# Two attention query jobs made a pair of block sums in a hybrid decoder step

## The chip, the cores and the metric

The kernel runs on one core of one Trainium2 chip. A core has a matrix engine (TensorE, PE in the profile), a vector engine (VectorE, DVE), a scalar engine (ScalarE, ACT), a general engine (GpSimd, POOL) and a sync engine (SP) that issues most transfers. The metric is the device time of one execution in microseconds. Of the kernel before, three runs took 834.29, 834.73 and 835.82 us; the median is 834.73.

## The reference

One layer of a decoder with two branches is computed for a prompt of 1024 positions and for 8 samples of 4 positions each (32 sample positions). The width is 1024.

```python
h, gate = adaln_in(x, c, w_ada, b_ada, g_norm)          # normalised, conditioned rows
(mq, mk, mv, mi, mf, mo, mz, aq, ak, av, az, gm, ga) = split_in(h @ w_in)
y_m, C, n, m = mlstm_branch(mq, mk, mv, mi, mf, mo, mz, C0, n0, m0, b_i, b_f, g_mn)
q = partial_rope(aq.reshape(B, T, A_HEADS, A_HEAD_DIM), pos)
...
o = attn_prompt(q, k, v, sinks)     # window of 128, 8 query heads on 2 key heads of 64
y_a = o.astype(x.dtype) * jax.nn.silu(az)
u = jax.nn.sigmoid(gm) * (y_m @ w_mo) + jax.nn.sigmoid(ga) * (y_a @ w_ao)
x = x + gate * (u @ w_o)
```

The first branch has four heads of 128 with a matrix memory that is carried over chunks of 128 positions. The second is attention over a sliding window. Samples attend to a cache and have memories of their own. All data is float32, and the outputs are the rows, the states and the kept keys and values.

## The kernel before, in words

**Products in three parts.** Every large product of float32 is made from a high and a low part of both operands, in the form float32r: high by high, high by low, low by high. Weights are split into `wh` and `wl` when they have been loaded: ACT copies the high part and DVE subtracts.

**Plain jobs.** A plain job (`job`, with `job_part` and `piece`) makes 128 columns of `h @ w_in` for all 1056 positions. It takes the positions in pieces of 384, 384 and 288 and, for each, eight blocks of the inner dimension, three matmuls for each block. The list `order` says which jobs are plain: keys and values of attention (`ak`, `av`), its four query groups (`aq` 0 to 3), then the first head's `mq`, `mk`, `mv` and the second head's `mq`, and at the end of the kernel the products with `w_mo`. `queries(g)` is the plain job of a query group: its evacuation scales by 0.125, applies the rotation and stores the queries in DRAM (`qD`), and the last piece also fills the samples' queries in `qpad`.

**Pairs.** All other columns of `w_in` are made two jobs at a time (`Pair`, `block_products`). The two jobs' weights are four blocks and the prompt's rows are four blocks, and seven products of sums of such blocks replace eight. Each product is 4 blocks of the inner dimension x 3 matmuls of 512 columns. The sums of the rows' blocks (`t1` to `t4`) are formed once by the generator `sum_blocks`; the sums of weights' blocks are formed for each pair by DVE (`first_sums`, `split`). The products go in the order 1, 6, 2, 7, 5, 3, 4 in the first pair, and 5, 6, 2, 7, the next pair's 1, 3, 4 in the others. They accumulate in PSUM banks (`X`, `W`, `Y`, `Z`); product 6 goes on a bank `bw` that ACT has filled with a copy of the result of product 1, and products 7 and 4 on a bank `by`. Each finished quarter goes to `evac` of the pair's kind. The 32 samples are done apart: 16 small matmuls `smp` and one `smpo`. The kinds are `head_in` (4 pairs), `gate` (8), `query_gate` (2) and `head_gate` (4).

**Side work.** Between the matmuls of jobs and pairs, `side.tick()` lets in work of other kinds. Each kind is a generator that yields where it has to wait: the units of attention (`unit(g, b0)`, 16 of them, stream "a"; each has a visit of scores `sc`, one of transposes `pt` and one of outputs), the heads of the matrix memory (`head`, stream "m"), the samples' attention and heads (`sample_attention`, `sample_head`, stream "s"), the sums of blocks (stream "x"), and conditioning gates and output weights (`ada_gate`, `out_weights`, stream "g"). `Side` keeps a modelled time, and starts a step when its time has come and its class of PSUM banks has been free long enough. The banks are of four classes, g, a, b and o, two each; units take their scores' banks from a beside plain jobs and from o beside pairs.

**Order.** The order on TensorE is written out by hand: each matmul and transpose has a dependency on the one before (`mm` and `tr` call `in_order`). In the part of the program that matters here, DVE and ACT are placed by a scheduler, and then keep their queue's order. Transfers go out on SP's queue in the order of the program, stores some time after their data.

**Samples' heads.** After each second head, `sample_head` sums the partial results of two heads. It multiplies them with a constant (`C_S32`, 32 columns) into a bank `st`, copies the 32 rows, normalises, transposes each head into one half of a bank `sty`, and multiplies it into `gs`:

```python
for i, (g, _) in enumerate(tails):
    tr(ty[:, i], ns[:, i, 0:128], ident[:NS, :NS])
    V.tensor_scalar(gs[:, g], ty[:, i], gmn[:, g:g + 1], None, op0=ALU.mult)
```

**Output weights.** `out_weights` multiplies the rows of `w_out` with the gate and forms sums of blocks of them for the end of the kernel; it is started by `hook` at product 6 of the pair of number `OUT_WEIGHTS`, which is the second gate pair.

Of the kernel before, what the change touches and what calls it, by code (L numbers as in the profile page):

```python
# [14 lines left out]
AF = mybir.ActivationFunctionType  # L15
ALU = mybir.AluOpType
# [5 lines left out]
SEQ = 1024  # L22
NB = 8
NT = 4
NS = NB * NT
T = SEQ + NS
PITCH = 1088
NH = 4
# [4 lines left out]
KT = D // 128  # L33
# [4 lines left out]
C_END = 849  # L38
# [135 lines left out]
def body(tc, a):  # L174
    nc = tc.nc
    with ExitStack() as ctx:
# [11 lines left out]
        def pb(shape, name):  # L188
            return ps.tile(shape, F32, tag="b", bufs=2, name=name)

        def po(shape, name):
            return ps.tile(shape, F32, tag="o", bufs=2, name=name)

        def ht(shape, name, dt=F32):
            return sp.tile(shape, dt, tag="half", bufs=50, name=name)

        def sm(shape, name, bufs=3, dt=F32):
            return sp.tile(shape, dt, tag=name, bufs=bufs, name=name)
# [45 lines left out]
        def store(out, in_):  # L244
            due.append((side.now + 8.0, out, in_))
# [8 lines left out]
        def dma(out, in_, late=False):  # L254
            stores(in_.tensor)
            issue(out, in_, late)
# [10 lines left out]
        def mm(out, lhsT, rhs, start, stop, share=1, more=False):  # L267
            n = int(np.prod(rhs.shape[1:]))
            side.now += max(n, 250) / 2400 if rhs.dtype == F32R else max(n * 4 // share, 128) / 2400
            side.products += 1  # L270
            in_order(nc.tensor.matmul(out, lhsT, rhs, start=start, stop=stop, skip_group_check=more))  # L271

        def tr(out, in_, idn):
            side.now += 0.11
            side.products += 1
            in_order(nc.tensor.transpose(out, in_, idn))  # L276
# [43 lines left out]
        cst = cp.tile([128, C_END], F32, name="cst")  # L320
# [243 lines left out]
        order = []  # L564
# [345 lines left out]

        def sample_attention():
            qpad, vns, kTs = at["qpad"], at["vns"], at["kTs"]
            kc, vc = ([ht([128, 4, 128], f"{n}{u}") for u in range(2)] for n in ("kc", "vc"))
            smask = ht([128, 2, WIN + NS], "smask")
            sinkr = cp.tile([128, 1], F32, name="sinkr")
            for u in range(2):
                dma(kc[u], a["cache_k"][:, 4 * u:4 * u + 4])
                dma(vc[u], a["cache_v"][:, 4 * u:4 * u + 4])
            dma(smask, a["smask"])
            dma(sinkr, a["sink_rows"])  # L920
            yield 12.0, "b"
            for u in range(2):
                tq = pb([128, 4, 128], f"kctp{u}")
                for j in range(4):
                    tr(tq[:, j], kc[u][:, j], ident)
                S.copy(kc[u], tq)
                yield 3.0, "b" if u == 0 else "o"
            sc = po([128, 2, WIN + NS], "scs")
            for u in range(2):
                for w in range(4):  # L930
                    b = u * 4 + w
                    qb = qpad[:, b].rearrange("p k g t -> p (k g t)")
                    r = slice(32 * w, 32 * w + 32)
                    mm(sc[r, u, 0:WIN], qb, kc[u][:, w], start=True, stop=True)
                    mm(sc[r, u, WIN:], qb, kTs, start=True, stop=True)
            p = ht([128, 2, WIN + NS], "ps")
            mx = cp.tile([128, 2], F32, name="mxs")
            for u in range(2):
                V.tensor_tensor_reduce(p[:, u], sc[:, u], smask[:, u], 1.0, sinkr, ALU.add, ALU.max,
                                       accum_out=mx[:, u:u + 1])  # L940
            nmx = cp.tile([128, 4], F32, name="nmxs")
            V.tensor_scalar(nmx[:, 0:2], mx, -1.0, None, op0=ALU.mult)
            V.tensor_scalar(nmx[:, 2:4], nmx[:, 0:2], sinkr, None, op0=ALU.add)
            den = cp.tile([128, 2], F32, name="dens")
            for u in range(2):
                S.activation(p[:, u], p[:, u], AF.Exp, bias=nmx[:, u:u + 1], accum_out=den[:, u:u + 1])
            S.activation(nmx[:, 2:4], nmx[:, 2:4], AF.Exp)
            V.tensor_tensor(den, den, nmx[:, 2:4], op=ALU.add)
            V.reciprocal(den, den)
            for u in range(2):  # L950
                V.tensor_scalar(p[:, u], p[:, u], den[:, u:u + 1], None, op0=ALU.mult)
            yield 10.0, "b"
            pt = pb([128, 4, 128], "pts")
            for u in range(2):
                tr(pt[:, u], p[:, u, 0:WIN], ident)
                tr(pt[:NS, 2 + u], p[:, u, WIN:], ident)
            pT = kc[0]
            S.copy(pT[:, 0:2], pt[:, 0:2])
            V.tensor_copy(pT[:NS, 2:4], pt[:NS, 2:4])
            yield 7.0, "o"  # L960
            o = po([128, 2, 128], "os")
            for u in range(2):
                for w in range(4):
                    r = slice(32 * w, 32 * w + 32)
                    mm(o[r, u], pT[:, u, r], vc[u][:, w], start=True, stop=False, share=4)
                for w in range(4):
                    r = slice(32 * w, 32 * w + 32)
                    mm(o[r, u], pT[:NS, 2 + u, r], vns, start=False, stop=True, share=4)
            S.copy(p[:, :, 0:128], o)
            yield 4.0, "b"  # L970
            ot = pb([128, 2, 128], "ost")
            for u in range(2):
                tr(ot[:, u], p[:, u, 0:128], ident)
            for u in range(2):
                v4 = lambda t: t.rearrange("p (w k g t) -> p w k g t", k=2, g=4, t=NT)
                for kv, r in enumerate(half_rows):
                    V.tensor_copy(osm[r, :, 16 * u:16 * u + 16].rearrange("p g (w t) -> p w g t", t=NT), v4(ot[r, u])[:, :, kv])
            samples_done.append("a")


        yhD = [dp.tile([128, SEQ], F32, name=f"yhD{h}") for h in range(NH)]
# [54 lines left out]
        mD = [[dp.tile([128, SEQ], F32, name=f"{n}D{h}") for n in "qkv"] for h in range(NH)]  # L1036

        def head(h):
            an, wend, dec, fl = st["an"], st["wend"], st["dec"], st["fl"]
            C = [None]  # L1040
            w_ = {}
# [133 lines left out]
        def sample_head(h):  # L1175
# [64 lines left out]
                return  # L1240
            yield 3.0, "o"
            tot = po([128, 2, 129], f"st{h}")
            for i, (_, n4) in enumerate(tails):
                mm(tot[:NS, i], cst[:, C_S32:C_S32 + NS], n4, start=True, stop=True)
            ns = z[:NS, 0:258].rearrange("p (m e) -> p m e", e=129)
            S.copy(ns, tot[:NS])
            ssq = sm([NS, 2], "sssq", 2)
            for i in range(2):
                jk = sm([128, 128], "mjk", 2, BF16)
# [6 lines left out]
            for i in range(2):  # L1256
                V.tensor_scalar(ns[:, i, 0:128], ns[:, i, 0:128], d[:, i:i + 1], r[:, i:i + 1], op0=ALU.mult, op1=ALU.mult)
            yield 4.0, "b"
            ty = pb([128, 2, NS], f"sty{h}")
            for i, (g, _) in enumerate(tails):  # L1260
                tr(ty[:, i], ns[:, i, 0:128], ident[:NS, :NS])
                V.tensor_scalar(gs[:, g], ty[:, i], gmn[:, g:g + 1], None, op0=ALU.mult)
                samples_done.append(g)
            tails.clear()
            if h == NH - 1:
# [159 lines left out]
        def ahead(self, key, src, th):  # L1425
            self.held[key] = o = ht([128, 512], "ho")
            dma(o, src[:, HALF[th]])

        class head_in:
            names = lambda i: paired[i]  # L1430
            ahead = lambda self, i: None
# [155 lines left out]
                    W = filled(pg, "bw", X, j)  # L1587
                side.tick()

        order += [("ak", 0), ("av", 0)] + [("aq", g) for g in range(4)]  # L1590
        inner = [(n, h) for h in range(NH) for n in ("mq", "mk", "mv")]
        paired = list(zip(inner[4::2], inner[5::2]))
        order += inner[:4]
# [411 lines left out]
                    summed("t4", k, b21, t2, ALU.subtract)  # L2005
                    yield 2.4, ""

        pairs = [Pair(head_in, i) for i in range(len(paired))] + [Pair(gate, d) for d in range(KT)] + [Pair(query_gate, i) for i in range(2)] + [Pair(head_gate, h) for h in range(NH)]

        def hook(n, i):  # L2010
            if n == 0 and i in (6, 5):
                side.until(lambda: {6: "t2", 5: "t1"}[i] in formed)
            if i == 6:
                if pairs[n].kind is query_gate:
                    side.until(lambda: len(units_done) == 16)
                side.until(lambda: len(samples_done) >= {head_in: 0, gate: 0, query_gate: 1, head_gate: pairs[n].i + 2}[pairs[n].kind])
            if (n, i) == (OUT_WEIGHTS, 6):
                side.add("g", out_weights())
            if (n, i) in LOADS:
                side.add("x", att_sums(LOADS.index((n, i))))  # L2020
            if n == len(pairs) - 1:
                next(att, None)

        OUT_WEIGHTS = 5
        LOADS = [(len(pairs) - 2, 7), (len(pairs) - 1, 5)]
        work = block_products(pairs, hook)
        att = att_products()
        side.add("g", ada_gate())
        side.add("x", sum_blocks())
        blocks["t1"] = block(0, 1)  # L2030
        for g in range(4):
            queries(g)
        side.add("s", sample_attention(), "b")
        for h in range(NH):
            head_jobs(h)

# [337 lines left out]
```

## Time and profile before

| | |
|---|---|
| median of three runs | 834.73 us |
| the profiled execution | 832.12 us |
| its span, first to last instruction | 830.4 us |
| mean granted clock of TensorE | 0.997 |
| TensorE busy | 810.4 us |
| VectorE busy | 593.8 us |
| ScalarE busy | 420.5 us |
| share of the DMA engines' time, main queue | 54.1% |

Rows of the timeline have the start in microseconds, the duration, the engine and line, the operation with its tiles (out<-in) and, where the engine was idle before, for how long and what released it. Matmuls overlap: the distance of two starts is what one costs. Almost all matmuls stand on line 271 and all transposes on line 276, since helpers issue them; tiles tell them apart. A group's row has count, busy time, mean duration in ns and the idle time before it.

The main stages are: loading and normalising first, plain jobs up to about 209 us, the eighteen pairs up to about 640 us, then the output products of attention, the plain jobs with `w_mo` (690 to 735 us) and the final rows.

### The profile page before, as it was taken

The page shows a single profiled execution, that of the slowest core. Times are in us where ns is not written, and L with a number is a line of the kernel's source. Part 1 is how long each engine was busy: PE and PEld are TensorE (multiplying, and loading weights), DVE is VectorE, ACT ScalarE, POOL GpSimd, SP SyncE. Part 2 cuts the span into 40 slices and gives each one's busy share as a digit, 9 for nine tenths or more (in the row PEclk, how much of TensorE's full clock was granted, in tenths as well). Part 3 has the DMA queues.
Part 4 walks back from the last instruction along what each step waited for, and adds up shares of the span by engine and source line. Part 5 has one row for each costly group of instructions (what it writes and reads, how often), then busy time and mean ns, then how long its engine had stood idle before and what let it go on. Part 6 is the DMA issues. An engine that isn't in the chain of part 4 may idle for free. (4 is left out here: it accounts for less than half of the span.)

```text
span 830.4 us, 15038 instructions
## 1 busy us (share of the span) xinstructions
PE 810.4 (98%) x5129; PEld 669.3 (81%) x5129; DVE 593.8 (72%) x1479; ACT 420.5 (51%) x1030; POOL 67.2 (8%) x128
## 2 busy tenths in 40 slices
PE   6999999999999999999899999999999999999996
PEld 3779897888788788888788877887888789997775
DVE  4889886656656456475577785897569988974776
ACT  5664365555474564555455453544346654334343
POOL 0120000000000001000001000000002104250000
PEclk9999999999999999999999999999999999999998
DMA  9997766356436425479856345464336785643633
GB/s 334 378 357 238 184 201 213 118 150 217 143 111 189 114 85 150 140 240 286 268 188 205 120 141 155 143 203 142 103 117 196 230 288 172 212 146 122 202 109 108
DMA packets 106689, 153.96 MB, mean 185 GB/s; under 512 B 20448, under 2 KB 54368, under 8 KB 106580
## 3 DMA queue, kind: packets, MB, share of 16 engines
q1 hardware_dynamic: 100964, 142.25, 54.1%
q10 hardware_dynamic: 4176, 6.56, 2.2%
q0 software_dynamic: 1472, 4.20, 1.4%
q8 instruction: 40, 0.66, 0.3%
q14 instruction: 37, 0.30, 0.1%
HBM read 109.22 MB, written 44.75 MB: 185 GB/s over the span
## 5 line engine op out<-in xcount | busy, mean ns | idle before, releaser
L220 ACT ACTIVATE p<-p,nmx 128x256 f32<-128x256 f32 (+1 forms) x64 | 31.0, 486 | 12.4 <-DVE nmx L220 12.1
L271 PE MATMUL g_aq<-h_h,wh_aq 128*128 128x384 f32 (+1 forms) x96 | 32.2, 336 | 0.0
L271 PE MATMUL g_aq<-h_h,wl_aq 128*128 128x384 f32 (+1 forms) x96 | 30.9, 322 | 0.0
L271 PE MATMUL g_aq<-h_l,wh_aq 128*128 128x384 f32 (+1 forms) x96 | 30.8, 321 | 0.0
L271 PE MATMUL g_w_mo<-ym_l,wh_w_mo 128*128 128x384 f32 (+1 forms) x96 | 30.8, 321 | 0.0
L271 PE MATMUL g_w_mo<-ym_h,wh_w_mo 128*128 128x384 f32 (+1 forms) x96 | 30.8, 321 | 0.0
L271 PE MATMUL g_w_mo<-ym_l,wl_w_mo 128*128 128x384 f32 (+1 forms) x96 | 30.8, 321 | 0.0
L220 DVE CUSTOM_DVE_ANT_0 p<-sc,cst,sink 128x256 f32<-128x256 f32 (+1 forms) x64 | 26.2, 464 | 5.3 <-PE sc L271 5.2
L259 POOL DMA_DIRECT2D oD<-uqv x16 | 8.9, 554 | 183.2 <-ACT uqv L220 161.0
L220 DVE COPY p<-pt 128x512 f32<-128x512 f32 (+1 forms) x16 | 10.5, 657 | 13.6 <-PE pt L276 13.6
L271 PEld LDWEIGHTS g_aq<-h_h,wh_aq 128*128 128x128 f32 x96 | 18.0, 188 | 2.5 <-issue 1.5
L271 PEld LDWEIGHTS g_w_mo<-ym_l,wh_w_mo 128*128 128x128 f32 x96 | 18.0, 188 | 0.0
L271 PEld LDWEIGHTS g_aq<-h_l,wh_aq 128*128 128x128 f32 x96 | 18.1, 188 | 0.0
L271 PEld LDWEIGHTS g_w_mo<-ym_h,wh_w_mo 128*128 128x128 f32 x96 | 18.0, 188 | 0.0
L271 PE MATMUL sc<-ukv,uqv 64*128 64x256 f32 (+1 forms) x128 | 18.0, 390 | 0.0
L271 PEld LDWEIGHTS g_aq<-h_h,wl_aq 128*128 128x128 f32 x96 | 18.0, 188 | 0.0
L271 PEld LDWEIGHTS g_w_mo<-ym_l,wl_w_mo 128*128 128x128 f32 x96 | 18.0, 188 | 0.0
L220 ACT ACTIVATE p<-p,den 128x256 f32<-128x256 f32 (+1 forms) x32 | 14.5, 491 | 5.7 <-DVE den L220 5.6
L220 ACT ACTIVATE sq<-rows_h 128x512 f32<-128x512 f32 (+2 forms) x14 | 8.2, 582 | 17.8 <-issue 12.0
L220 DVE TENSOR_TENSOR et<-et,S 128x384 f32<-128x384 f32 (+1 forms) x12 | 6.1, 510 | 15.4 <-PE S L271 12.7
L271 PE MATMUL g_mq<-h_h,wh_mq 128*128 128x384 f32 (+1 forms) x48 | 16.8, 349 | 0.3 <-ACT mk L220 0.3
L276 PE MATMUL pt<-cst,p 128*128 128x128 f32 x120 | 16.4, 277 | 0.5 <-DVE mx L220 0.5
(2073 smaller groups left out, 2841.4 us busy)
## 6 DMA issues: line engine op xcount, KB each, us to landing
x<-xT SPq DMA_DIRECT2D x16, 256.0 KB, 5.6
early_h<-w_ada SPq DMA_DIRECT2D x8, 512.0 KB, 9.0
adar_ga<-w_ada SPq DMA_DIRECT2D x16, 256.0 KB, 4.0
wr_ga<-w SPq DMA_DIRECT2D x16, 256.0 KB, 2.9
wr_gm<-w SPq DMA_DIRECT2D x16, 256.0 KB, 3.6
taD<-gt SPq DMA_DIRECT2D x16, 256.0 KB, 2.2
tmD<-gt SPq DMA_DIRECT2D x16, 256.0 KB, 5.3
wor<-w_out SPq DMA_DIRECT2D x16, 256.0 KB, 5.1
```

Source lines behind the costliest of these rows:

```text
L220: ins = f(*args, **kw)
L259: ins = (eng or nc.sync).dma_start(out, in_)
L271: in_order(nc.tensor.matmul(out, lhsT, rhs, start=start, stop=stop, skip_group_check=more))
L276: in_order(nc.tensor.transpose(out, in_, idn))
```

## The change

Query groups 2 and 3 are no longer plain jobs. They are the first pair of a new kind, `att_in`, whose evacuation adds, shuffles, multiplies with 0.125 and the rotation's tables and stores the queries; it loads four tables of 128 x 512 for that. When both halves of a group are stored, its four units are added to the stream, so they come beside pairs. The samples' attention is started from this pair, waits until four units are done, loads the cached values later, and limits how many units run at a time to two while it runs and to three after it. A `head` waits until its gates' values exist and `t1` has been formed. In `sample_head` the state sums take 104 columns of the constant (`C_S32` to `C_END`) instead of 32, the copy takes 104 rows, and both transposes are issued before both evacuations. `OUT_WEIGHTS` goes from 5 to 8; as one pair has been put in front, that is from the second gate pair to the fourth.

```diff
 def sample_attention():
-    kc, vc = ([ht([128, 4, 128], f"{n}{u}") for u in range(2)] for n in ("kc", "vc"))
+    while len(units_done) < 4:
+        yield 1.0, ""
+    side.streams["a"]["max"] = 2
+    kc = [ht([128, 4, 128], f"kc{u}") for u in range(2)]
...
+    vc = [ht([128, 4, 128], f"vc{u}") for u in range(2)]
+    for u in range(2):
+        dma(vc[u], a["cache_v"][:, 4 * u:4 * u + 4])
     yield 10.0, "b"
...
     samples_done.append("a")
+    side.streams["a"]["max"] = 3

 def head(h):
+    while not st or "t1" not in formed:
+        yield 1.0, ""

 # sample_head
     tot = po([128, 2, 129], f"st{h}")
+    w = C_END - C_S32
     for i, (_, n4) in enumerate(tails):
-        mm(tot[:NS, i], cst[:, C_S32:C_S32 + NS], n4, start=True, stop=True)
-    ns = z[:NS, 0:258].rearrange("p (m e) -> p m e", e=129)
-    S.copy(ns, tot[:NS])
+        mm(tot[:w, i], cst[:, C_S32:C_END], n4, start=True, stop=True)
+    nw = z[:, 0:258].rearrange("p (m e) -> p m e", e=129)
+    S.copy(nw[:w], tot[:w])
+    ns = nw[:NS]
...
-    ty = pb([128, 2, NS], f"sty{h}")
+    ty = pb([128, 2, 128], f"sty{h}")
+    for i in range(2):
+        tr(ty[:, i, 0:w], nw[:w, i, 0:128], ident[:w, :w])
     for i, (g, _) in enumerate(tails):
-        tr(ty[:, i], ns[:, i, 0:128], ident[:NS, :NS])
-        V.tensor_scalar(gs[:, g], ty[:, i], gmn[:, g:g + 1], None, op0=ALU.mult)
+        V.tensor_scalar(gs[:, g], ty[:, i, 0:NS], gmn[:, g:g + 1], None, op0=ALU.mult)

+class att_in:
+    names = lambda i: (("aq", 2 * i), ("aq", 2 * i + 1))
+
+    def ahead(self, i):
+        if i == 6:
+            tables.extend([ht([128, 512], f"turn{th}{j}") for j in range(2)] for th in range(2))
+            at["turn"] = ht([128, 2, NS], "turns")
+            dma(at["turn"], a["rope"][:, :, SEQ:T])
+            for th in range(2):
+                for j in range(2):
+                    dma(tables[th][j], a["rope"][:, j, HALF[th]])
+
+    def evac(self, c, th, *src):
+        g = 2 * self.i + c
+        x, t = ht([128, 512], "aq"), ht([128, 512], "aqr")
+        if len(src) == 2:
+            V.tensor_tensor(x, src[0], src[1], op=ALU.add)
+        else:
+            S.copy(x, src[0])
+        V.stream_shuffle(t, x, shuf)
+        for y, f in zip((x, t), tables[th]):
+            V.scalar_tensor_tensor(y, y, 0.125, f, op0=ALU.mult, op1=ALU.mult)
+        V.tensor_tensor(x, x, t, op=ALU.add)
+        store(qD[g][:, HALF[th]], x)
+        self.held[c] = self.held.get(c, 0) + 1
+        if self.held[c] == 2:
+            for b0 in (0, 2, 4, 6):
+                side.add("a", unit(g, b0))
+
+    def samples(self, o):
...
+        side.add("s", sample_attention(), "b")

-order += [("ak", 0), ("av", 0)] + [("aq", g) for g in range(4)]
+order += [("ak", 0), ("av", 0)] + [("aq", g) for g in range(2)]

-pairs = [Pair(head_in, i) for i in range(len(paired))] + ...
+pairs = [Pair(att_in, 1)] + [Pair(head_in, i) for i in range(len(paired))] + ...

-OUT_WEIGHTS = 5
+OUT_WEIGHTS = 8
-for g in range(4):
+for g in range(2):
     queries(g)
-side.add("s", sample_attention(), "b")
```

More of the change, by code (lines that the diff above doesn't have):

```diff
@@ L917, in sample_attention @@
                 dma(kc[u], a["cache_k"][:, 4 * u:4 * u + 4])
-                dma(vc[u], a["cache_v"][:, 4 * u:4 * u + 4])
             dma(smask, a["smask"])
@@ L1427, in ahead @@
             dma(o, src[:, HALF[th]])
+        class att_in:
[25 more added lines that the diff above has]
+            def samples(self, o):
+                x, t = sm([128, 2, NS], "gts", 2), sm([128, 2, NS], "gts", 2)
+                S.activation(x, o, AF.Copy, scale=0.125)
+                V.stream_shuffle(t, x, shuf)
+                for y, j in ((x, 0), (t, 1)):
+                    V.tensor_tensor(y, y, at["turn"][:, j:j + 1].to_broadcast((128, 2, NS)), op=ALU.mult)
+                v3 = lambda y, r, c: y[r, c].rearrange("p (b t) -> p b t", t=NT)
+                for c in range(2):
+                    for kv, r in enumerate(half_rows):
+                        V.tensor_tensor(at["qpad"][r, :, kv, 2 * self.i + c], v3(x, r, c), v3(t, r, c), op=ALU.add)
+                side.add("s", sample_attention(), "b")
+        tables = []
         class head_in:
@@ L2006, in out_weights @@
                     yield 2.4, ""
-        pairs = [Pair(head_in, i) for i in range(len(paired))] + [Pair(gate, d) for d in range(KT)] + [Pair(query_gate, i) for i in range(2)] + [Pair(head_gate, h) for h in range(NH)]
+        pairs = [Pair(att_in, 1)] + [Pair(head_in, i) for i in range(len(paired))] + [Pair(gate, d) for d in range(KT)] + [Pair(query_gate, i) for i in range(2)] + [Pair(head_gate, h) for h in range(NH)]
         def hook(n, i):
@@ L2015, in hook @@
                     side.until(lambda: len(units_done) == 16)
-                side.until(lambda: len(samples_done) >= {head_in: 0, gate: 0, query_gate: 1, head_gate: pairs[n].i + 2}[pairs[n].kind])
+                side.until(lambda: len(samples_done) >= {att_in: 0, head_in: 0, gate: 0, query_gate: 1, head_gate: pairs[n].i + 2}[pairs[n].kind])
             if (n, i) == (OUT_WEIGHTS, 6):
```

## The prediction

> **What bounds the kernel now.** I read the page's busy times first, then TensorE's waits, then the timeline of PE around each of them.
>
> ```profile
> span 830.4 us, 15038 instructions
> PE 810.4 (98%) x5129; PEld 669.3 (81%) x5129; DVE 593.8 (72%) x1479; ACT 420.5 (51%) x1030; POOL 67.2 (8%) x128
> ```
>
> TensorE is busy for 98% of the span; nothing else is near. The profiled execution took 832.12 us, 1.7 us of it outside the span, and lies 2.6 us under the median of the runs, 834.73. My sum is made against 832.12 and its difference is then put on the median. Two things can change the end: what the matmuls themselves cost, and the few microseconds in which TensorE waits.
>
> ```profile
> PE xc L271 <- ACT xsq L220: 6.2, 1, 6.2
> PE S L271 <- DVE C L220: 2.3, 1, 2.3
> PE sty L276 <- DVE gs L220: 1.1, 2, 0.8
> ...
> PE pt L276 <- DVE mx L220: 0.5, 1, 0.5
> PE g_mq L271 <- ACT mk L220: 0.3, 1, 0.3
> ```
>
> The columns are microseconds in all, times, the longest. The first wait lies at the beginning, which the change does not touch. All others together are under 7 us, so a gain over some 5 us can only come out of the matmuls.
>
> **Part 1: two plain jobs become seven products.** A plain job is 8 k x 3 products over pieces of 384, 384 and 288 columns, so two are 96 matmuls of 384 columns and 48 of 288. The pair is 7 x 12 = 84 matmuls of 512 columns, and 17 instructions for the samples. Since matmuls overlap, a matmul's price is its pitch, start to start, not its duration.
>
> ```profile
> 102.96 0.29 PE L271 MATMUL g_aq<-h_h,wh_aq 128*128 128x288 f32 x1
> ...
> 103.88 0.29 PE L271 MATMUL g_aq<-h_l,wh_aq 128*128 128x288 f32 x1
> ...
> 111.54 0.33 PE L271 MATMUL g_aq<-h_l,wh_aq 128*128 128x384 f32 x1
> ...
> 112.23 0.34 PE L271 MATMUL g_aq<-h_h,wl_aq 128*128 128x384 f32 x1
> 112.50 1.14 PE L271 MATMUL sc<-ukv,uqv 64*128 64x256 f32 x8
> 113.56 0.44 PE L271 MATMUL g_aq<-h_h,wh_aq 128*128 128x384 f32 x1
> 113.84 0.34 PE L271 MATMUL g_aq<-h_l,wh_aq 128*128 128x384 f32 x1
> ```
> ```profile
> 307.79 0.39 PE L271 MATMUL bx<-h_h,wl_phead_in__3688 128*128 128x512 f32 x1
> ...
> 308.48 0.39 PE L271 MATMUL bx<-h_h,wl_phead_in__3688 128*128 128x512 f32 x1
> 308.70 0.33 PE L271 MATMUL smpo<-cst,smps 128*128 128x64 f32 x2
> ...
> 309.97 0.49 PE L271 MATMUL n<-hv,et 128*128 128x129 f32 x2
> ```
>
> 288 columns: seven pitches between 102.96 and 103.88, 0.131 each (0.1317 over a longer stretch). 384: four between 111.54 and 112.23, 0.173. 512: three between 307.79 and 308.48, 0.230. Out go 96 x 0.1735 + 48 x 0.1317 = 22.98 us, in come 84 x 0.2295 = 19.28, and the samples' block, 308.70 to 309.97, 1.27. Part 1 gives -2.4.
>
> Around a visit of scores the pitch is 0.27 on entry and 0.28 on return instead of 0.173: about 0.2 us for going into that form and back. By the changed order, float32r work is broken 132 times instead of 123; the total of side work is the same. Nine breaks at 0 (most added ones have full 128 rows, as the transposes) to 0.2 give 0 to +1.8; I take +0.4.
>
> Here a page speaks against the change. The Trainium skill, "TensorEngine Tiling (Array Packing)", section Key Properties, says that changing the tiling mode drains TensorE; by it each of the scores' 64-row visits pays, and with nine more such breaks the sum would be 1.4 us higher. The 0.27 and 0.28 agree in direction.
>
> **Part 2: the samples' state sums over 104 columns.** Before, the second transpose of `sty` stands behind the first evacuation:
>
> ```profile
> 516.46 0.24 PE L276 MATMUL sty<-cst,sz 32*128 32x32 f32 x1
> 517.04 0.24 PE L276 MATMUL sty<-cst,sz 32*128 32x32 f32 x1 [0.35 <-DVE gs L220]
> ...
> 579.32 0.24 PE L276 MATMUL sty<-cst,sz 32*128 32x32 f32 x1
> 580.33 0.24 PE L276 MATMUL sty<-cst,sz 32*128 32x32 f32 x1 [0.77 <-DVE gs L220]
> ```
>
> The pitches are 0.58 and 1.01. Both transposes are now issued first; one behind another costs about 0.11 (four in the 0.42 us from 290.21 to 290.63, below). That gives -(0.47 + 0.90) = -1.4. The four `st` matmuls stream as many columns as before, and their copy takes 104 rows in one instruction: nothing taken, as ACT at 51% hides it; without that cover a copy costs 0.3 to 0.6 (`bw` 0.58, below). Lower bound: no gain, if an evacuation then holds the bank elsewhere; upper, 1.6.
>
> **Part 3: stalls that go because the order around them changes.**
>
> ```profile
> 404.27 0.38 PE L276 MATMUL tv<-cst,hv 128*128 128x128 f32 x2
> 406.99 0.71 PE L271 MATMUL S<-hq,hk 128*128 128x128 f32 x4 [2.33 <-DVE C L220]
> ```
> ```profile
> 404.91 0.56 DVE L220 TENSOR_TENSOR et<-et,cst 128x384 f32<-128x384 f32 x1 [2.33 <-DMA tmD<-gt]
> 406.11 0.56 DVE L220 TENSOR_TENSOR qw<-qw,hq 128x384 f32<-128x384 f32 x1 [0.64 <-DMA qw<-wid]
> ```
>
> At 404 a head group's loads (`et`, `qw`) come late; DVE stands still for 2.33 us on them, and `C`, which `S` needs for its bank, is queued behind. It is the group whose loads were issued closest ahead of use; in the changed order none has so short a lead, so -2.5 (pitch 2.72 instead of 0.22). Upper end 0: another group is late in the same way. The wait of `g_mq` goes with the jobs that stood before it: -0.3, or 0.
>
> **Part 4: what the move adds.** Half of the units (16 in all; 11 or 12 now end beside pairs, 7 before) lose the plain jobs' banks and take those marked "o". There are three places.
>
> ```profile
> 289.05 0.66 PE L276 MATMUL pt<-cst,p 128*128 128x128 f32 x4
> 290.21 0.66 PE L276 MATMUL pt<-cst,p 128*128 128x128 f32 x4 [0.51 <-DVE mx L220]
> 290.63 0.47 PE L271 MATMUL bw<-h_h,wh_phead_in__3529 128*128 128x512 f32 x1
> ```
>
> (a) Where scores are directly followed by a unit's transposes, that unit waits for DVE's maximum of the scores before: 0.67 us of excess here (1.16 between the two rows, 0.49 of work). This stands once in the old order and three times in the new, once with a samples' softmax ahead on DVE: 0.67 + 1.35 + 0.67 less 0.67 is +2.0 if none is hidden; +1.4 taken, since visits that have other work before them in the same stop lose part of it. From 0 to +2.0.
>
> (b) Before `pt` of the units that run beside the output-gate sums of the conditioning, TensorE has 4.3 us of its own, DVE 5.1 to do on the same bank: 0 to +1.5, +0.7 taken.
>
> (c) Output weights (`out_weights`) start beside the fourth gate pair instead of the second. There they meet the samples' first heads. DVE runs its queue in order, so the sum `gt` of a gate pair stands behind all that is ahead of it; ACT then does the tanh, and only after it the copy `bw`, on which the next pair's product 6 accumulates:
>
> ```profile
> 447.43 0.63 ACT L220 ACTIVATE gt<-gt 128x512 f32<-128x512 f32 x1 [0.28 <-DVE gt L220]
> 447.96 0.58 ACT L220 COPY bw<-bx 128x512 f32<-128x512 f32 x1
> ```
> ```profile
> L220 DVE TENSOR_TENSOR wor<-wor,gb 128x512 f32<-128x512 f32 x16 | 11.0, 685 | 0.0
> L220 DVE TENSOR_TENSOR vf<-sz,wm 32x387 f32<-32x387 f32 (+1 forms) x12 | 6.0, 503 | 0.2
> L220 DVE TENSOR_TENSOR vm<-vf,vm 32x388 fp32r<-32x388 f32 (+1 forms) x12 | 5.9, 506 | 0.3
> L220 DVE TENSOR_TENSOR Cs<-Cs,sxb 128x387 f32<-128x387 f32 (+1 forms) x12 | 5.5, 511 | 0.0
> L220 DVE TENSOR_TENSOR gt<-p,bw 128x512 f32<-128x512 f32 x8 | 5.5, 688 | 7.2 <-PE bw L271 7.1
> ```
>
> In the new order of DVE some thirty instructions stand between the sum before and the one at the end of the sixth gate pair (three `vf` and three `vm` with their casts, three `Cs`, three `wor`, two `wost`, the weights' splits and a head's group): 14.7 us by these durations, with 9% of handovers 16.0, and tanh and copy 1.3 behind it. TensorE's work in that stretch is about 15, so product 6 of the seventh waits 2.3. Below: 0 (on the old order's rows DVE waited for PE here, 7.1 us in eight times); above: 4.5, if the group's loads are late. I take +2.3. At the other gate pairs the queue is shorter than TensorE's work.
>
> The sum: -2.4 + 0.4 - 1.4 - 2.5 - 0.3 + 1.4 + 0.7 + 2.3 = -1.8 us on the profiled 832.12, so 830.3, and 832.9 on the median. The new class's four loads of rotation tables (256 KB each) are issued on SP's queue ahead of the pair's product 6 and needed after product 2, that is 2 x 12 x 0.2295 = 5.5 us and some side work later.
>
> ```profile
> x<-xT SPq DMA_DIRECT2D x16, 256.0 KB, 5.6
> wr_ga<-w SPq DMA_DIRECT2D x16, 256.0 KB, 2.9
> ```
>
> Loads of that size land in 2.9 to 5.6 us, so they are hidden; if late, it is DVE that waits for them, and TensorE only when the bank of product 2 is wanted again, a product later (2.75 us). The stores of queries, four instead of six, stand on the same queue and nobody waits for them but the units' loads.
>
> **Rivals.** What a measurement here can tell from no change is about 0.2%, 1.7 us.
>
> A, slower: the queue of DVE at the gates. It is the mechanism of (c) with a higher price. Without (c) the sum is -4.1, so it decides from 5.8 us of waits. It speaks for it that 24 products of output weights (16 `wor`, 8 `wost`, 16.5 us at 0.685) fall on five pairs that already carry the samples' heads, (6.0 + 5.9 + 5.5) / 4 = 4.4 us of `vf`, `vm` and `Cs` for each head; against it, DVE at 72% overall. If that place waits 4.5 and its two neighbours 1.5 each, 7.5, the time is 834.73 - 4.1 + 7.5 = 838.1. The Trainium skill, "PSUM — Partial Sum Buffer", says that the queues of VectorE and ScalarE are strictly first in, first out; the rows at 404, where `C` stands behind `et`, agree.
>
> B, no change: the gain of part 3 does not come, since another group of a head is as late as that at 404. The sum without its 2.5 is +0.7, so 835.4; with half of it, 834.2.
>
> C, larger gain: the waits of (a), (b) and (c) are hidden by slack that an order without times does not show. The sum is -6.2 with none, -4.1 with (a) and (b) alone: 828.5 to 830.6, say 829.8.
>
> D, the change does not move units: the order shows otherwise (11 instead of 7), so it has no chance of its own.
>
> **How the numbers follow.** My forecast (a gain of 0.5 to 3.5 us) has 0.40, A 0.25, B 0.15, C 0.20. The forecast itself is 832.9, its own range 831.2 to 834.2. The whole range reaches down to 829.3 (C less its best fifth) and up to 838 (A's price): 829.3 to 838.0. Faster by over 0.2%, under 833.06: 0.27 of the forecast's 0.40 and all of C, 0.47. Within: 0.13 of the forecast and 0.11 of B, 0.24. Slower: A and 0.04 of B, 0.29.
>
> **What would show it.** In the profile after: 96 fewer matmuls of 384 columns in `g_aq` at 0.17 pitch; no wait of `sty` on `gs`; no wait of `S` on `C` over 1 us; `pt` waiting on `mx` two or three times, 0.5 to 1.0 each; one wait of `bw` on ACT's `bw` of 1 to 4 us between the sixth and the seventh gate pair, with DVE busy without a break before it. The prediction fails if `bw` waits at several gate pairs, if `S` waits again, or if the first pair's blocks are late, which would show as a wait of its matmuls on the block sums.

## The result, and the profile after

The changed kernel takes 843.5 us (median of four runs, 842.47 to 844.33) against 834.84 for the kernel before in as many; the ratio is 1.0114, with an interval of 1.0097 to 1.013. It is slower by 8.7 us, where a gain to 832.9 was forecast, and above 838.0, the upper end of the range. The profiled execution took 843.63, 11.5 more than the 832.12 of before, which lies 2.7 under that kernel's median; the account below is of these two executions.

TensorE does as much as before and waits more. First the page's span and busy times, then TensorE's waits (in all, times, longest):

```profile
span 841.9 us, 15008 instructions
PE 811.0 (96%) x5103; PEld 664.8 (79%) x5103; DVE 595.6 (71%) x1482; ACT 422.8 (50%) x1034; POOL 69.0 (8%) x128
```
```profile
PE bw L271 <- ACT bw L220: 7.0, 3, 5.4
PE xc L271 <- ACT xsq L220: 7.0, 1, 7.0
PE pt L276 <- DVE mx L220: 5.0, 3, 3.4
PE pt L276 <- DVE gb L220: 1.4, 1, 1.4
PE smp L271 <- ACT yt L220: 1.3, 1, 1.3
```

The waits of `S`, `sty` and `g_mq` are gone. In their place stand a wait of 5.4 us for the copy into `bw`, one of 3.4 for a unit's maxima, and three of 1.0 to 1.4 (another for a unit's maxima, one for `gb`, one for `yt`). All lines of the table together are 23.5 us, before 12.7: 10.8 of the 11.5.

The two long waits cost more in this execution than they show. The timeline of TensorE around the longest, and the table by stretches (busy of PE, PEld, DVE, ACT, POOL, then the granted clock, the DMA share and GB/s):

```profile
480.89 0.39 PE L271 MATMUL bz<-h_h,wl_pgate__5509 128*128 128x512 f32 x1
486.67 0.80 PE L271 MATMUL bw<-t2h,wh_pgate__5573 128*128 128x512 f32 x1 [5.40 <-ACT bw L220]
487.27 0.63 PE L271 MATMUL bw<-t2l,wh_pgate__5573 128*128 128x512 f32 x1
487.69 0.63 PE L271 MATMUL bw<-t2h,wl_pgate__5574 128*128 128x512 f32 x1
...
489.40 0.90 PE L271 MATMUL U<-hv,hk 128*128 128x129 f32 x4
```
```profile
486.00:488.00 2.00, 1.33 (x3) 1.13 (x4) 0.89 (x2) 1.62 (x4) 0.00 (x0) 0.65 0.77 284
488.00:490.00 2.00, 2.00 (x7) 1.61 (x7) 0.00 (x0) 0.00 (x0) 0.00 (x0) 0.50 0.90 335
490.00:492.00 2.00, 2.00 (x12) 1.67 (x11) 0.70 (x2) 0.51 (x1) 0.00 (x0) 1.00 0.02 5
```

After the wait the granted clock is 0.50 for some 3 us, and a matmul of 512 columns takes 0.42 instead of 0.23. The six up to 489.40 take 2.73 instead of 1.38, and the eight from 340.02 to 343.43, after the other long wait, 3.41 instead of 1.84: 2.9 us together. So 11.5 = 10.8 + 2.9 and a remainder of -2.2, in which the pair and its breaks lie.

What was late? DVE's timeline before the late sum at 485, and before the other one at 337:

```profile
480.06 0.69 DVE L220 TENSOR_TENSOR wor<-wor,gb 128x512 f32<-128x512 f32 x1
...
481.57 0.68 DVE L220 TENSOR_TENSOR wost<-wor,wor 128x512 f32<-128x512 f32 x1
...
483.59 0.68 DVE L220 TENSOR_TENSOR wost<-wor,wor 128x512 f32<-128x512 f32 x1
484.19 0.69 DVE L220 TENSOR_TENSOR wor<-wor,gb 128x512 f32<-128x512 f32 x1
484.79 0.68 DVE L220 TENSOR_TENSOR gt<-p,bw 128x512 f32<-128x512 f32 x1
```
```profile
337.36 0.69 DVE L220 TENSOR_TENSOR gt<-p,bw 128x512 f32<-128x512 f32 x1 [4.24 <-DMA yhD<-yt]
337.96 0.68 DVE L220 TENSOR_TENSOR wl_pgate__4079<-wr_ga,wh_pgate__4078 128x512 fp32r<-128x512 f32 x1
338.56 0.47 DVE L220 CUSTOM_DVE_ANT_0 p<-sc,cst,sink 128x256 f32<-128x256 f32 x1
```

At 485 the sum `gt` of the sixth gate pair stands behind a samples' head and output weights; it reads the bank into which ACT then copies `bw`. At 337 the same sum of an earlier pair holds DVE for 4.24 us with nothing to do: by the releaser, its new tile can be written only when the store of a `yt`, which had that space, has landed (the run with sums in place, below, bears this out). The maxima of a unit stand behind it. Both sums write a new half tile (a buffer of 128 x 512 on the chip), of which the kernel has 50.

### The profile page after: what moved, and what is told of

It reads as the page before. It is cut to its first block, busy times and chain, and to the rows that moved or that the text cites. A ratio compares the mean times of both kernels' runs of the same rounds, so it can differ in the third digit from the quotient of the medians.

```text
span 841.9 us, 15008 instructions
## 1 busy us (share of the span) xinstructions
PE 811.0 (96%) x5103; PEld 664.8 (79%) x5103; DVE 595.6 (71%) x1482; ACT 422.8 (50%) x1034; POOL 69.0 (8%) x128
## 5 line engine op out<-in xcount | busy, mean ns | idle before, releaser
L276 PEld LDWEIGHTS pt<-cst,p 128*128 128x128 f32 x120 | 13.6, 141 | 9.4 <-DVE mx L220 4.5
L220 ACT ACTIVATE gt<-gt 128x512 f32<-128x512 f32 (+2 forms) x19 | 10.9, 572 | 12.2 <-DVE gt L220 11.2
L271 PE MATMUL g_aq<-h_h,wh_aq 128*128 128x384 f32 (+1 forms) x48 | 16.0, 333 | 0.0
L220 DVE SCALAR_TENSOR_TENSOR tgw_mo<-tgw_mo,g_w_mo 128x384 f32<-128x384 f32 (+1 forms) x24 | 12.2, 515 | 5.3 <-PE g_w_mo L271 5.3
L271 PEld LDWEIGHTS sc<-ukv,uqv 64*128 64x128 f32 x128 | 10.6, 186 | 6.5 <-issue 3.3
L271 PE MATMUL g_mq<-h_h,wl_mq 128*128 128x384 f32 (+1 forms) x48 | 15.5, 322 | 0.0
L271 PE MATMUL g_aq<-h_h,wl_aq 128*128 128x384 f32 (+1 forms) x48 | 15.4, 322 | 0.0
```

The lines of the kernel that those rows point to most:

```text
L220: ins = f(*args, **kw)
```

## The experiments

### The bank freed by ACT

Theory at this point: DVE's queue is too long, and the bank is freed too late.

```diff
 class gate: evac
-    t = tanh_of(self, src, "gt")
+    if (c, th) == (0, 1):
+        t = ht([128, 512], "gt")
+        S.copy(t, src[1])
+        V.tensor_tensor(t, t, src[0], op=ALU.add)
+        S.activation(t, t, AF.Tanh, scale=0.5)
+    else:
+        t = tanh_of(self, src, "gt")
```

> Edit of the changed kernel: at the end of each gate pair's product 3, ACT copies the bank `bw` to `gt` first, and DVE adds from the copy, so that the bank is free without DVE. Theory (the sum `gt` is late in DVE's queue behind the samples' head and the output weights, and the bank it reads is the one the next product 6 needs): the wait of `bw` at 481 us falls from 5.4 to under 1 us, the halved clock after it (about 1.9 us) goes too, 843.5 becomes about 836.5. Rival (product 6 waits for its weights or for loads that are late): the wait stays over 4 us and the time within 1 us of 843.5.

841.64 us (ratio to before 1.0095, 1.0068 to 1.0122). Missed: the wait of `bw` is still 4.3 us, though ACT no longer waits for DVE's sum. TensorE's wait, and ACT's timeline, which tells what ACT does wait for:

```profile
PE bw L271 <- ACT bw L220: 5.9, 3, 4.3
```
```profile
483.38 0.58 ACT L220 COPY gt<-bw 128x512 f32<-128x512 f32 x1 [2.66 <-DVE wost L220]
484.00 0.57 ACT L220 COPY bw<-bx 128x512 f32<-128x512 f32 x1
```

The copy waits for `wost`, an instruction on quite other data. The only thing that ties them is the space: `gt` takes the half tile of an output weight, and `wost` is its last reader. So neither expectation held: not DVE's place for the sum alone, and not the weights of product 6, but a free half tile.

### No transposes straight after scores

```diff
 Side.tick
-    used |= banks
+    used |= banks | ({"b"} if "+" in banks else set())
```

> Edit of the changed kernel: a stop of side work that takes scores on the banks o takes no step with banks b after it, so transposes never follow scores directly. Theory (the transposes wait for DVE's maxima of the scores just before): the waits of `pt` at 223, 278 and 336 us (1.2, 0.7, 3.6 us and 1.6 us of halved clock behind the last) go, 843.5 becomes about 836.5. Rival (DVE itself is held at 336 us by a tile's space that is released only when a store of `yt` to `yhD` has landed, 4.2 us): the wait at 336 goes over to another instruction, only the 1.9 us of the other two are won, about 841.5.

840.17 us (1.0085, 1.0056 to 1.0114). The waits of TensorE:

```profile
PE bw L271 <- ACT bw L220: 7.0, 3, 5.4
...
PE pt L276 <- DVE gb L220: 1.4, 1, 1.4
PE pt L276 <- DVE mx L220: 1.2, 1, 1.2
```

The waits at 223 and 278 are gone, and the third has 1.2 us left, without slow clock. The time lies between the two expectations, 3.3 us under 843.5, a difference that the two intervals do not separate. The waits are clearer: those of `pt` on `mx` fall from 5.0 to 1.2 us. So the order of scores and transposes was part of the price; the sum at 336, which still waits 4.1 us for the store of a `yt`, was another.

### Output weights later

```diff
-OUT_WEIGHTS = 8
+OUT_WEIGHTS = 12
```

> Edit of the changed kernel: OUT_WEIGHTS 12 instead of 8, so no output weights fall between the sixth and the seventh gate pair. Theory: there the queue of DVE ahead of `gt` is shorter by two `wor` and two `wost`, 2.5 to 3 us, so the wait of `bw` falls from 5.4 to 2.5 to 3 us and the halved clock goes; 843.5 becomes about 839, if no such place arises later. Rival (the samples' head alone makes it late): the wait stays over 4.5 us; 842 to 844.

838.57 us (1.0052, 1.0031 to 1.0072).

```profile
PE pt L276 <- DVE mx L220: 5.0, 3, 3.4
PE bw L271 <- DVE wl_phead_gate__6698 L220: 2.1, 1, 2.1
PE bw L271 <- DVE wor L220: 1.7, 1, 1.7
...
PE bw L271 <- ACT bw L220: 0.7, 1, 0.7
```

The wait of 5.4 us is gone altogether, not halved as a shorter queue would have it; what is left of that kind is the 0.7 of the first pair. Two waits of 2.1 and 1.7 come up later, where the output weights now are. The time of 839 was met in part by luck: more went than expected at 481, and 3.8 us came back elsewhere. Here the same work has a price at either place.

### Only the samples' sums, in the kernel before

```diff
 # the kernel before, sample_head
-    mm(tot[:NS, i], cst[:, C_S32:C_S32 + NS], n4, start=True, stop=True)
+    mm(tot[:w, i], cst[:, C_S32:C_END], n4, start=True, stop=True)
...
+    for i in range(2):
+        tr(ty[:, i, 0:w], nw[:w, i, 0:128], ident[:w, :w])
```

> Edit of the kernel before: only the part on the samples' state sums (104 columns, 104 rows copied, both transposes issued before both evacuations). Theory: the two waits of `sty` on `gs` go, 1.3 to 1.4 us; ratio 0.9984 to 0.9983. Rival (more columns and rows cost what the waits save): ratio 1.000.

831.3 us, ratio 0.9966 (0.9952 to 0.998): 2.8 us less, the interval reaching from 1.7 to 4.0. `sty` no longer stands among the waits. The forecast of 1.4 lies just outside. The start-to-start distances show some 0.46 us more, as the samples' four visits (two of `st`, two of `sty`) no longer have a small shape (see the last section); what the rest is stays open.

### Sums in place

The new theory: space. `p5` is read for the last time by the last sum of a pair, so the sum can be written over it and needs no new half tile.

```diff
 class Pair: done
+    self.own = (c, th) == (0, 1) and self.kind.__name__ in ("gate",)
 tanh_of
-    t = ht([128, 512], name)
+    t = src[0] if self.own else ht([128, 512], name)
```

> Edit of the changed kernel: at the last use of `p5` in a gate pair the sum `gt` is written over `p5` instead of into a new half tile; nothing else. Theory (the 50 half tiles are all in use: the sum stands late because its tile's space comes free late, at 335 us with the landing of a store of `yt`, at 481 us with the last reader of an output weight): the wait of `pt` at 336 us falls from 3.4 to at most 1.4 us, that of `bw` at 481 from 5.4 to under 1, both without halved clock, and 843.5 becomes about 834.5 (2.0 + 4.5 + 1.6 + 1.9 less, 833.5 to 835.5). Rival (DVE's queue is simply too long there): the wait at 481 stays over 3 us, and 843.5 becomes 839 to 841.

834.57 us, where 834.5 was expected (1.001, 0.9994 to 1.0026): with one tile fewer for each gate pair the loss against the kernel before is gone. TensorE's waits, and DVE's timeline at the place that was worst:

```profile
PE pt L276 <- DVE mx L220: 3.7, 3, 2.1
PE smp L271 <- ACT yt L220: 1.7, 1, 1.7
PE bw L271 <- ACT bw L220: 1.6, 2, 0.9
PE pt L276 <- DVE gb L220: 1.4, 1, 1.4
```
```profile
473.27 0.55 DVE L220 TENSOR_TENSOR vf<-sz,wm 32x387 f32<-32x387 f32 x1
473.75 0.67 DVE L220 TENSOR_TENSOR p<-p,bw 128x512 f32<-128x512 f32 x1
474.45 0.35 DVE L220 CAST vm<-vf 32x388 fp32r<-32x388 f32 x1
```

The sum is now the instruction between `vf` and `vm`, some eighteen places earlier in DVE's queue: the scheduler had put it late because its space came free late. The samples' head and the output weights are all still there. The wait at 336 became 2.1 us, more than the 1.4 expected; there DVE's sum now stands at 333.94 and waits for TensorE alone, but the scores' tile `p` behind it waits 1.47 us for the same store of `yt`, so the shortage itself is not over. Nor did the halved clock go at this place, as was expected: the granted clock is 0.50 for 3.4 us from 338.5 on. At 481 more was won than expected (the wait is gone; the 0.9 left is at 571), so that the sum of the forecast agrees so closely is in part luck.

### The same in the kernel before

```diff
 # the kernel before, with 104 columns
+    self.own = (c, th) == (0, 1) and self.kind.__name__ in ("gate", "query_gate", "head_gate", "head_in")
```

> The kernel before with the part on the samples' state sums, and with the last sum of every pair written over `p5` (gates, query gates, head gates, head inputs). Theory (the wait of `S` at 404 us, 2.3 to 3.2 us in the two looks, comes from a half tile that a store of a gate releases late): it falls under 1 us; ratio to the kernel before 0.9966 less 0.003, about 0.994. Rival (a late load of its own): the wait stays over 2 us, ratio 0.9966 as without this edit.

831.33 us, ratio 0.9959 (0.9947 to 0.9972), no different from the run without this edit. Missed: the wait of `S` at 404 did not fall. TensorE's wait, and DVE's row ahead of it:

```profile
PE S L271 <- DVE C L220: 3.6, 1, 3.6
```
```profile
406.99 0.56 DVE L220 TENSOR_TENSOR et<-et,cst 128x384 f32<-128x384 f32 x1 [4.25 <-DMA tmD<-gt]
```

### Both, and output weights again

```diff
 # the changed kernel, sums in place for all kinds of pairs but att_in, and
+    used |= banks | ({"b"} if "+" in banks else set())
 # second run also
-OUT_WEIGHTS = 8
+OUT_WEIGHTS = 12
```

> Edit of the changed kernel: both the sums over `p5` (all kinds of pairs) and no transposes straight after scores. Theory: the waits at 223, 278, 336, 481 us are gone, with the halved clock; left are `pt` at 146 us (1.4) and the first fill of `bw` (0.8); 843.5 less 1.2, 0.7, 5.2 and 7.3 is 829 to 831, under the kernel before. Rival (waits move on to the next place of the same banks): 833 or more.

> As the run with both edits, and OUT_WEIGHTS 12 instead of 8. Theory (with space for the sums the place of the output weights no longer decides): within 1.5 us of that run. Rival (the length of DVE's queue between the sixth and seventh gate pair decides): 2 us or more faster than that run.

828.86 us (0.9938, 0.9921 to 0.9955), just under the 829 to 831 of the theory, then 827.43 (0.9916, 0.9901 to 0.993). Of the first run's waits two over 1 us are left that the kernel before doesn't have; the first of them was not expected:

```profile
PE smp L271 <- ACT yt L220: 1.6, 1, 1.6
PE pt L276 <- DVE gb L220: 1.4, 1, 1.4
```

With output weights at 12 the wait of `smp` on `yt` is gone too; 1.4 us between the two runs, whose intervals overlap, is within the 1.5 that the theory allowed. Where there is space for the sums, the place of the output weights matters little, against 4.9 us without (843.5 to 838.57).

### The gate sums' bank, and what the pair itself is worth

```diff
 ada_gate
     V.tensor_scalar(gb, gb, 0.25, None, op0=ALU.mult)
+    side.free["b"] = side.now + 6.0
```

> As the run with sums in place, no transposes straight after scores and OUT_WEIGHTS 12; in addition the banks b are counted as taken for 6 modelled us after the output-gate sums `ada_ga`, so that the units' transposes come later than those sums' four additions on DVE. Theory (this is the price named as (b) in the prediction, a wait on the bank's readers): the wait of `pt` on `gb` at 146 us, 1.4 us, goes, and the halved clock that the profile of that run shows from 150 to 153 us with it; 827.4 becomes 825 to 826. Rival (another step takes the wait at the same place): 827 to 828.

825.52 us, ratio 0.9904 (0.9885 to 0.9923): the lowest median of all, 9 us under the kernel before. The wait of `pt` on `gb` is gone, and so is the halved clock in this profile; the 1.9 us against the run before are not clear of the intervals. All its waits of TensorE, beginning apart, are 0.7 or less:

```profile
PE xc L271 <- ACT xsq L220: 6.3, 1, 6.3
...
PE aw L271 <- ACT aw L220: 0.7, 2, 0.5
PE bw L271 <- ACT bw L220: 0.7, 1, 0.7
```

The counterpart has everything but the pair. (With one pair fewer in front, OUT_WEIGHTS 11 is the eighth gate pair here, the same place as 12 with the pair; the expectation below calls it the seventh.)

```diff
 # the kernel before, with 104 columns, sums in place,
 # no transposes after scores, the bank held, and
-OUT_WEIGHTS = 5
+OUT_WEIGHTS = 11
```

> The kernel before, without the pair of query jobs, with all that has been repaired since: 104 columns, sums over `p5`, no transposes straight after scores, banks b held after `ada_ga`, and output weights two pairs before the same place (OUT_WEIGHTS 11, the seventh gate pair). It tells what the pair itself is worth. Theory of the prediction (2.0 us for seven products with their breaks): this kernel is 2 us slower than the one with the pair and the same repairs, 827 to 828. Rival (the breaks by side work beside pairs take back the gain; by the starts of matmuls the two profiles at hand differ by 0.5 us without stalls): within 1 us of it.

832.26 us (0.9971, 0.9957 to 0.9985). The difference to 825.52 is 6.7, far more than either expectation. Most of it isn't the price of the products: this kernel has waits of its own that the other has not.

```profile
PE pt L276 <- DVE mx L220: 1.7, 1, 1.7
PE sc L271 <- ACT uqv L220: 1.2, 1, 1.2
```

The two profiled executions (830.34 and 825.08) differ by 5.3 us; their waits add up to 13.0 and 9.1, which is 3.9 of it. The 1.4 left is the pair's worth by these two runs; the starts of matmuls give 0.9 (below), and the 0.5 between is not accounted for. Why the medians differ by another 1.5 stays open too.

### What makes `S` wait in the kernel before

```diff
 # the kernel before, with 104 columns and sums in place
-OUT_WEIGHTS = 5
+OUT_WEIGHTS = 11
```

> The kernel before with 104 columns, sums over `p5` and OUT_WEIGHTS 11 instead of 5, nothing else. It tells where the wait of `S` at 404 us comes from, which sums in place did not take away. Theory (half tiles held by the rows of the output weights and stores of gates keep a head's `et` waiting): the wait of 3.6 us falls under 0.5, ratio 0.9959 less 0.004, 0.992. Rival (the load of `et` is late for another reason): the wait stays over 2 us, ratio 0.996.

832.73 us (0.9983, 0.9969 to 0.9996), not the 0.992 of the theory.

```profile
PE sty L276 <- DVE sz L220: 2.3, 1, 2.3
PE S L271 <- DVE C L220: 0.8, 1, 0.8
```
```profile
404.35 0.56 DVE L220 TENSOR_TENSOR et<-et,cst 128x384 f32<-128x384 f32 x1 [2.04 <-DMA et<-nmd]
```

The wait of `S` falls from 3.6 to 0.8, nearly as the theory has it, so it was the output weights' presence that made the head's `et` late there. DVE's row tells the same: `et` waited 4.25 us for the store of a gate with unrelated data, and now 2.04 for its own load. A wait of 2.3 at the samples' transposes takes its place, with the granted clock at 0.50 for 3.4 us behind it, and the time is no better.

## Why the prediction was wrong, point by point

**Part 1, the pair (-2.4 with +0.4 for breaks).** The pitches were right: without breaks 84 matmuls at 0.2275 instead of 96 at 0.1735 and 48 at 0.1315 is -3.9, and the samples' block +1.3. The nine more breaks were right too: 131 in the changed kernel, 122 before. Their price was mis-sized. From the distances between starts in the run with both edits, a break beside 512 columns costs 0.094 on the return and 0.025 on the entry, and a break beside plain jobs 0.102 and 0.056. That run has 100 and 34 of them, the kernel before 78 and 44; added up over all visits they take 17.3 us (the changed kernel as it was has the same) and 16.0. But the kernel before with the samples' sums over 104 columns alone has 15.6, so the pair's own breaks cost about +1.7 instead of +0.4, near the upper end of the range given, and the pair is worth about 0.9 us, not 2.0. That transposes break the stream for nothing was wrong: after visits in the full shape the first matmul still comes 0.086 late.

**Part 2, the samples' sums (-1.4).** Right in kind; measured 2.8, the interval from 1.7. The form of the visits was put at nothing; its change is worth some 0.46 of it.

**Part 3, the wait of `S` (-2.5) and of `g_mq` (-0.3).** Both went, as forecast. That the lead of the head's loads decided it was only half of the cause: the last run moves the output weights away from this place, as the change does, and the wait falls to 0.8.

**Part 4.** (a), scores before transposes, three times, +1.4 with 2.0 at most: the places were right and the first two measured 1.2 and 0.7 in the prediction's own measure, the excess of pitch (waits of 1.03 and 0.55). The third took 3.4 and 1.6 of slow clock, since the sum ahead of the maxima waited for the store of `yt`. (b), +0.7 with 1.5 at most, measured 1.4, and the run that holds the bank shows that this was it. (c) is the step that failed most: "+2.3", with 4.5 at most, became 5.4 and 1.4 of slow clock. The place, the chain from `gt` to the copy `bw` to product 6, and the work ahead on DVE were as written. But the working took the place of `gt` in DVE's queue as given, and the durations ahead of it as the price. (The 7.1 us of DVE waiting for PE that it sets against this are in seven waits by the table, not eight.) In its place the runs showed the half tiles: ACT without DVE was late too (4.3), and the sum over `p5` with all that work left in place was in time, eighteen places earlier. A wait that was not foreseen, `smp` for `yt`, 1.3, stayed with sums in place (1.7 and 1.6; ACT's `yt` waits there for the store of a gate) and is gone in the runs with output weights at 12, and in the one with the bank freed by ACT.

**Missing altogether: the clock.** The prediction counted waits as long as they last. In the profile after, the halved clock behind the two longest waits cost 1.6 and 1.4 us more.

**The rivals.** A, slower, had the right place, engine and direction with 0.25, and 838.1 as its time; its price lacked the third wait of (a) and the clock. The Trainium skill's rule under it, "PSUM — Partial Sum Buffer", section Engine vs sequencer instructions, that those queues are first in, first out, is borne out by the maxima behind `gt` at 337; but it says nothing on why the sum stands where it does. B and C fell. The signs named to look for were the right ones: no `sty`, no `S`, and `bw` between the sixth and seventh gate pair, though 5.4 where "1 to 4 us" stood, with DVE busy without a break over 0.2 us from 473 us until the sum.

Added up: the pair -0.9, the form of the samples' visits -0.5, `S`, `sty` and `g_mq` -3.7, the new waits of `bw`, `pt` and `smp` +13.5, the clock +2.9, the beginning +0.8, +0.2 of small lines, and a rest of -0.8 that no line names, is 11.5.

## What to carry to other kernels

Before a step is moved beside others, count the buffers it keeps alive there, not only the engines' time: an instruction that writes a new tile can be scheduled late, or stand at the head of an engine's queue, only because that tile's space is still held by a store or by a reader with unrelated data. A releaser in the timeline whose data have nothing to do with the waiting instruction (`gt` for `yhD<-yt`, a copy for `wost`) is the sign. The cure here was one tile fewer, by writing a result over its last-read operand (8.9 us), rather than another engine for the work (1.9 us, not clear of noise).

## What the runs showed of the hardware

**A wait can halve the clock, and its length does not tell whether it will.** In the profiles of this case the granted clock fell to 0.50 around waits of TensorE of 1.40, 2.10, 2.33, 3.23, 3.43, 3.44, 4.33 and 5.40 us. It stayed at 1.00 around others of 1.40, and of 2.33 (kernel before), 3.15 (the samples' sums alone) and 3.57 us (the same with sums in place). The longest that left the next matmuls at their usual pitch of 0.23, and one of 2.33 (output weights at 11) behind which they stand 0.42 apart:

```profile
408.33 0.71 PE L271 MATMUL S<-hq,hk 128*128 128x128 f32 x4 [3.57 <-DVE C L220]
408.80 0.47 PE L271 MATMUL bw<-t2h,wh_pgate__4785 128*128 128x512 f32 x1
409.11 0.39 PE L271 MATMUL bw<-t2l,wh_pgate__4785 128*128 128x512 f32 x1
409.34 0.39 PE L271 MATMUL bw<-t2h,wl_pgate__4786 128*128 128x512 f32 x1
```
```profile
579.05 0.48 PE L276 MATMUL sty<-cst,sz 104*128 104x104 f32 x2 [2.33 <-DVE sz L220]
...
579.62 0.62 PE L271 MATMUL bx<-h_l,wh_phead_gate__6795 128*128 128x512 f32 x1
580.04 0.63 PE L271 MATMUL bx<-h_h,wl_phead_gate__6796 128*128 128x512 f32 x1
```

The halved clock lasts 3.4 us each time, and twice 6.8 (around 3.23 with the bank freed by ACT, around 5.40 with no transposes after scores). In the run with OUT_WEIGHTS 12 and both edits a wait of 1.40, followed by scores, was enough (granted clock 0.50 from 150 to 152 us); in the run before it, with the same wait, the clock stayed at 1.00. What decides between such cases stays open; no run here varied the length of a wait alone.

```profile
150.00:152.00 2.00, 2.00 (x8) 1.25 (x5) 2.00 (x8) 0.87 (x2) 0.00 (x0) 0.50 0.59 171
```

**Small shapes cost on both sides of a visit.** In the run with both edits, means over all visits beside 512 columns: the matmul after a visit comes 0.085 to 0.089 late if the visit ended in 128 x 128 transposes or products, and 0.108 to 0.111 if it ended in scores (64 rows), a unit's outputs (64 columns) or samples (32 columns or rows). The visit itself starts 0.001 to 0.007 late in the full shape, and 0.090 to 0.095 in the small ones. The state sums at 104 columns and their transposes at 104 rows belong to the first kind (0.085 and 0.086, and 0.001 and 0.005), where at 32 they took 0.111 and 0.112, and 0.091, in the kernel before. That is 0.11 us for each visit that is widened. Two kinds stand apart: transposes of the samples' keys (`stk`, 128*32) start only 0.001 late, and after `sU` (96 rows) the next matmul comes only 0.010 late. The Trainium skill, "TensorEngine Tiling (Array Packing)", section Key Properties, says that a change of the tiling mode drains TensorE; the two groups of numbers agree with it, the start of `stk` does not.
